# Source order for TensorE and the sync DMA queue in the last four stages, and for all engines in gate and up

## The chip, the core and the metric

The kernel runs on one core of a Trainium2 chip. The core has a matrix engine (TensorE, PE; its weight loads are shown as PEld), a vector engine (VectorE, DVE), a scalar engine (ScalarE, ACT), a general engine (GpSimd, POOL), and a sync engine (SP) that issues DMAs; 16 DMA engines move the data. ScalarE can issue DMAs too. Every engine has its own instruction queue, and instructions wait on semaphores. TensorE's clock is granted at one of two levels, 1.2 and 2.4 GHz; the profile gives it as 0.5 to 1.0. The metric is the device time of one execution in microseconds, the median of several runs.

## The reference

One inference step of a one-layer encoder for 1024 frames of a new stream and 32 frames of a running one. `layer` does, for all 1056 token rows together:

```python
u = rmsnorm(x, norm_mix_g) @ w_in                       # 1024 -> 4616 columns
cy = silu(layernorm(depthwise_causal(a * sigmoid(gl)))) @ w_conv_pw
ao = attend(q, k, v, logf).reshape(B, T, 512) @ w_attn_o
mixed = sigmoid(g_conv) * cy + sigmoid(g_attn) * ao
h = x + mixed @ w_out                                   # 1024 -> 1024
z = rmsnorm(h, norm_ffn_g)
h = h + (silu(z @ w_gate) * (z @ w_up)) @ w_down        # 1024 -> 2816 -> 1024
```

and at the end a last rmsnorm. All inputs are float32.

## The kernel before

**Arithmetic.** Each float32 operand is kept as a rounded half "hi" (cast by ScalarE) and a difference "lo" (subtracted by VectorE or GpSimd; the helper is `split`, lines 237 and 240). A product is three matmuls: hi by hi, hi by lo, lo by hi.

**Stages.** (1) input projection, convolution, attention and `mixers` (the convolution's projection and its gate; results go to the DRAM tile `md`). (2) `attn_out`: attention's projection, 8 blocks of 128 output columns, each for 4 chunks of 264 token columns: 12 matmuls per block and chunk, then a multiplication by the gate read from `gd` (L1455), an addition of `md` (L1457), and a split into `mh`, `ml`. (3) `out_proj`: the output projection in two pairs of chunks, 8 blocks each; after a pair's blocks, `pair_operand` (a generator, advanced step by step) sums the squares by a matmul with ones (L1528), computes the norm (L1529 to L1535), scales h (L1547, four operations for each quarter), forms sums of quarters (L1555), and splits them into the seven operands `zh`, `zl` of that pair. (4) `ffn_up`: 22 units of 128 hidden columns. Gate and up of one unit are a two by two block product that is done as seven products (a Strassen-like scheme in the orders `ORDER` and `EARLY`), 12 matmuls of 264 columns each (L1603), 84 matmuls for a unit and pair, 3696 in all. The seven weight operands of the next unit are prepared beside it (`unit_weights`: a sum `ws`, L1577, then a split into `whl`). Unit 0 is done for pair 0 first and for pair 1 last. (5) `ffn_down`: the down projection, 352 columns a matmul, reading the hidden values back from `hidd`; its last part also writes the output rows.

**Seven products.** `ORDER` is 1, 5, 2, 6, 7, 3, 4; products 1, 5 and 2 are copied out of their PSUM banks by ScalarE (L1606) and their banks are used again by products 7, 3 and 4, so that product 7 waits for the copy of product 1. GpSimd adds two of the copies (L1609, L1610), VectorE adds the rest (L1612 to L1618); a Silu on ScalarE and a multiplication on VectorE (L1661 to L1664) finish each half, and a DMA writes it (L1666).

**What sets the order.** The instructions are traced in source order; a planner then orders each engine's queue by priorities and by the times that it expects, and places tiles in memory. `high_priority` moves instructions forward. Inside `manual_schedule(engines=...)` the named engines keep the source order. Before the change that holds for TensorE from attention up to the end of `mixers` (the `region` that `mixers` closes); from `tokens_in_pairs` on the planner orders every queue, with one matmul pinned by `keep_in_program_order` (L1528). Memory of stages 2 to 4 lies over that of stage 1, and stage 5's over that of 2 to 4, so a first tile of a stage may wait until an old one is given up.

**Buffers that matter.** Seven PSUM banks for products and one for the ones matmul in stages 2 to 4; pool `first` (14 tiles of 4 by 264 columns), `second` (16), `passing` (8 smaller ones); 4 + 6 tiles for weight operands; two tiles for the sums `ws`; four raw weight tiles, two of which (`raw`) stay across stages.

Of the kernel before, what the change touches and what calls it, by code (L numbers as in the profile page):

```python
# [15 lines left out]
P = 128  # L16
NP = 1024
# [38 lines left out]
EARLY = (1, 5, 7, 4, 3, 2, 6)  # L56
BANK = {1: "a", 5: "b", 2: "c", 6: "d", 7: "a", 3: "b", 4: "c"}
# [79 lines left out]
class Builder:  # L137
# [223 lines left out]
    def jobs(self):  # L361
# [951 lines left out]
    def mixers(self, region):  # L1313
# [5 lines left out]
        def gated(j):  # L1319
# [25 lines left out]
    def tokens_in_pairs(self):  # L1345
# [11 lines left out]
        self.start_queue([cols(rows(I["w_attn_o"][0]), j) for j in range(8)] +  # L1357
                         [cols(rows(I["w_out"][0]), j) for _ in range(2) for j in range(8)], 4)
# [57 lines left out]
    def attn_out(self):  # L1416
# [3 lines left out]
        self.fetch(3)  # L1420
        w = self.block()

        def loads(j):
            out = [self.Q(self.pa, s="gate") for _ in range(2)]
            for x, src in zip(out, (self.gd[1, j], self.md[j])):
                nc.sync.dma_start(x.rearrange("p c n -> p (c n)"), src)
            return out

        oh = {}
        for c in range(4):  # L1430
            x = self.Q(self.pa, s="o")
            e = min(CW, NP - CW * c)
            with self.tc.high_priority(400):
                nc.sync.dma_start(x[:, :, 0:e], self.od[:, :, CW * c:CW * c + e].rearrange("a p n -> p a n"))
            if e < CW:
                nc.vector.tensor_copy(x[:, :, e:CW], self.os)
            oh[c] = self.Q(self.pa, FR, "oh"), self.Q(self.pa, FR, "ol")
            self.split(x, *oh[c], nc.vector)
        x = None
        mx = {}  # L1440
        nxt = loads(0)
        for j in range(8):
# [4 lines left out]
            if (1, j) in late:  # L1447
                nc.scalar.activation(g, g, AF.Sigmoid)
            for p in range(2):
                if j % 2 == 0:  # L1450
                    mx[p, j // 2] = self.Q(self.pb, FR, "mh"), self.Q(self.pb, FR, "ml")
                for c in (2 * p, 2 * p + 1):
                    ps = self.psd()
                    self.block_products(ps, wj, lambda k: (oh[c][0][:, k, :], oh[c][1][:, k, :]), CW)
# [9 lines left out]
    def out_proj(self, w):  # L1464
# [53 lines left out]
        for self.unit in self.ahead:  # L1518
            pass
# [450 lines left out]
```

## Time and profile before

| | us |
|---|---|
| median of 3 runs | 1581.76 (1579.77 to 1582.91) |
| profiled execution, its own time | 1584.55 |
| its span, first to last instruction | 1582.8 |
| TensorE busy in the span | 1513.3 (96%) |
| weight loads | 1474.0 (93%) |
| VectorE busy | 1013.0 (64%) |
| ScalarE busy | 594.7 (38%) |
| GpSimd busy | 509.7 (32%) |
| granted clock, mean | 0.986 |

The profile is of one execution. Busy times of the engines overlap. A matmul's end is modelled, and matmuls overlap in the records, so that an interval between starts says more than a duration. A wait is the idle time of an engine before an instruction, with what released it in brackets. The stages of the change lie between about 657 us and the end.

### The profile page before, as it was taken

What the parts mean: (1) busy time and instruction counts of PE and PEld (TensorE: products, weight loads), DVE (VectorE), ACT (ScalarE), POOL (GpSimd) and SP (SyncE); (2) the same over time, 40 slices, a digit from 0 to 9 for tenths busy, and PEclk for the clock granted to TensorE, in tenths of its full rate; (3) what the DMA queues carried; (4) which work ended last, traced back from release to release, by engine and by line L of the source; (5) the groups of instructions that cost most, each with busy time, mean ns of one, the idle gap of its engine ahead of it and who ended that gap; (6) DMA issues with size and microseconds to landing.
All of it is one profiled execution on the core that took longest, in us unless ns stands there. A gap on an engine that the chain in (4) does not pass through costs nothing.

```text
span 1582.8 us, 27182 instructions
## 1 busy us (share of the span) xinstructions
PE 1513.3 (96%) x10622; PEld 1474.0 (93%) x10622; DVE 1013.0 (64%) x1742; ACT 594.7 (38%) x1220; POOL 509.7 (32%) x473
## 2 busy tenths in 40 slices
PE   8999999989999999899997999999999989999997
PEld 7999998979999998789997999999999989999996
DVE  7799998668776565267499655555555545442226
ACT  4412212376655444243455333333333334121115
POOL 2200000433432221210004566676666661122221
PEclk9999999999999999989999999999999999999999
DMA  8312332434634377685641222222222228321113
GB/s 249 119 41 80 91 100 78 122 88 136 196 106 114 109 239 221 193 261 166 181 140 44 79 82 78 78 77 65 70 81 82 81 75 324 111 83 51 42 63 110
DMA packets 209711, 186.18 MB, mean 118 GB/s; under 512 B 12587, under 2 KB 186567, under 8 KB 209584
## 3 DMA queue, kind: packets, MB, share of 16 engines
q1 hardware_dynamic: 209567, 184.46, 37.6%
q8 instruction: 83, 1.36, 0.3%
q14 instruction: 45, 0.36, 0.1%
q10 hardware_dynamic: 16, 0.00, 0.0%
HBM read 131.41 MB, written 53.01 MB: 117 GB/s over the span
## 4 chain that ended last, share of the span: by engine, by line
PE 56%; DVE 10%; POOL 5%; ACT 4%; issue 3%; DMA 2%; SPq 0%; ACTq 0%; DVEq 0%; POOLq 0%
PE pd L1413 18%; PE pd L1603 17%; PE pd L418 11%; POOL whl L240 4%; DVE ws L1577 2%; PE po L1101 2%; PE ps L1062 2%; PE pt L1084 2%; PE pd L1751 1%; DVE h L1547 1%; POOL t L1609 1%; PE pt L243 1%; DVE zl L240 1%; ACT whl L237 1%; PE pd L1776 1%
## 5 line engine op out<-in xcount | busy, mean ns | idle before, releaser
L1603 PE MATMUL pd<-zh,whl 128*128 128x264 f32 x2464 | 457.4, 286 | 15.0 <-ACT t L1606 7.3
L1603 PEld LDWEIGHTS pd<-zh,whl 128*128 128x128 f32 x2464 | 384.8, 189 | 19.9 <-ACT t L1606 11.6
L1603 PE MATMUL pd<-zl,whl 128*128 128x264 f32 x1232 | 351.1, 285 | 0.6 <-DVE zl L240 0.6
L418 PE MATMUL pd<-xl,whi 128*128 128x352 f32 x832 | 270.6, 325 | 0.5 <-POOL xl L528 0.5
L418 PE MATMUL pd<-xh,whi 128*128 128x352 f32 x832 | 271.0, 326 | 0.0
L418 PE MATMUL pd<-xh,wlo 128*128 128x352 f32 x832 | 270.9, 326 | 0.0
L1603 PEld LDWEIGHTS pd<-zl,whl 128*128 128x128 f32 x1232 | 233.0, 189 | 0.9 <-DVE zl L240 0.9
L240 POOL TENSOR_TENSOR wlo<-raw,whi 128x640 fp32r<-128x640 f32 (+2 forms) x55 | 102.9, 1872 | 244.3 <-ACT whi L237 194.6
L240 POOL TENSOR_TENSOR whl<-ws,whl 128x512 fp32r<-128x512 f32 x105 | 143.5, 1382 | 114.0 <-ACT whl L237 114.0
L237 ACT CAST whi<-raw 128x1024 fp32r<-128x1024 f32 (+2 forms) x78 | 70.2, 900 | 235.6 <-PE pd L1413 111.2
L418 PEld LDWEIGHTS pd<-xl,whi 128*128 128x128 f32 x832 | 156.8, 188 | 1.9 <-POOL xl L528 0.8
L418 PEld LDWEIGHTS pd<-xh,whi 128*128 128x128 f32 x832 | 156.8, 189 | 1.4 <-issue 0.2
L418 PEld LDWEIGHTS pd<-xh,wlo 128*128 128x128 f32 x832 | 156.8, 188 | 0.7
L755 DVE SCALAR_TENSOR_TENSOR acc<-cu,wdw,acc 128x1024 f32<-128x1024 f32 x120 | 147.2, 1278 | 0.2
L1727 DVE TENSOR_TENSOR h<-pd,h 128x352 f32<-128x352 f32 x96 | 49.8, 522 | 134.7 <-PE pd L1413 134.3
L1413 PE MATMUL pd<-hl,whi 128*128 128x352 f32 x360 | 116.1, 323 | 0.0
L1413 PE MATMUL pd<-hh,whi 128*128 128x352 f32 x360 | 116.1, 322 | 0.0
L1413 PE MATMUL pd<-hh,wlo 128*128 128x352 f32 x360 | 116.1, 322 | 0.0
L237 ACT CAST whl<-ws 128x512 fp32r<-128x512 f32 x115 | 71.2, 620 | 96.0 <-DVE ws L1577 70.4
L1609 POOL TENSOR_TENSOR t<-t,t 128x264 f32<-128x264 f32 x44 | 43.6, 991 | 165.5 <-ACT t L1606 165.5
L1046 POOL TENSOR_SCALAR_AFFINE_SELECT cr<-cr 128x128 f32<-128x128 f32 x64 | 25.7, 401 | 160.7 <-DVE s L1069 83.2
L948 POOL TENSOR_TENSOR v<-vt,v 128x256 fp32r<-128x256 f32 x16 | 12.0, 772 | 201.3 <-DVE v L947 201.3
(341 smaller groups left out, 3133.4 us busy)
## 6 DMA issues: line engine op xcount, KB each, us to landing
raw<-in_w_in SPq DMA_DIRECT2D x35, 512.0 KB, 4.0
hidd<-y SPq DMA_DIRECT2D x44, 264.0 KB, 2.0
hid<-hidd SPq DMA_DIRECT2D x18, 528.0 KB, 4.3
gd<-gate SPq DMA_DIRECT2D x48, 176.0 KB, 1.8
q<-qd SPq DMA_DIRECT2D x32, 256.0 KB, 5.1
raw<-in_w_down SPq DMA_DIRECT2D x24, 320.0 KB, 3.3
raw<-in_w_gate SPq DMA_DIRECT2D x12, 512.0 KB
raw<-in_w_up SPq DMA_DIRECT2D x12, 512.0 KB
```

Of the source, the lines that this page charges most:

```text
L237: nc.scalar.copy(hi, src)
L240: (lo_engine or nc.gpsimd).tensor_tensor(lo, src, f32(hi), ALU.subtract)
L418: nc.tensor.matmul(ps[:, :n], lhs, b, start=(m == 0), stop=(m == total - 1))
L755: nc.vector.scalar_tensor_tensor(acc[:, 0:NP], cu[:, j:j + NP], w(j), acc[:, 0:NP], op0=ALU.mult, op1=ALU.add)
L1062: nc.tensor.matmul(s[:, 512 * j:512 * j + e - o], q[:, m, qs], k[:, o:e], start=(m == 0), stop=(m == 1))
L1084: nc.tensor.transpose(t[:, o:o + P], lt[n, b][:, P * kb:P * kb + P], self.ident)
L1101: nc.tensor.matmul(o[:, 0:256], self.v[p][hh][:, kb, :], pt[:, m, r:r + 256], start=(kb == 0 and m == 0), stop=(kb == 2 * g + 1 and m == 1))
L1413: self.nc.tensor.matmul(ps[:, :n], a[:, k, :], b, start=(m == 0), stop=(m == total - 1))
L1577: nc.vector.tensor_tensor(src, q(terms[0]), q(terms[1]), terms[2])
L1603: nc.tensor.matmul(banks[b], x[:, k, :], y[:, k, :], start=first and k == m == 0, stop=last and k == 3 and m == 2, skip_group_check=True)
L1609: nc.gpsimd.tensor_tensor(t2, t2, t5, ALU.add)
L1727: nc.vector.tensor_add(s, ps[:, :CH], s)
```

## The change

It has five parts. (a) From `tokens_in_pairs` to the end, TensorE and SP keep the source order; in `ffn_up` all five engines do. (b) `attn_out` issues the four loads of attention's output first, takes three weight blocks at once, and goes through the chunks in the outer loop for those three blocks; the other five blocks go as before. Its first two weight blocks are loaded at the end of `mixers`, as two further entries of the list `L`; `dense` looks one block ahead for splits and three for loads, so it also splits block 0 and loads block 2, which `attn_out` then does again. (c) The last `md` writes (block 7) and the last `hidd` write are issued by ScalarE. (d) The preparation of a unit's weights is cut into steps `s` (the sum) and `p` (the split), placed between the seven products by the tables `STEPS`, and stands ahead of the copies and additions of the product just issued; the operands of pair 1 are advanced one step later than before. (e) Silu and multiplication stand right behind the products that they need.

```diff
+STEPS = {0: "s0", 1: "p0", 2: "s3", 3: "p3", 4: "s4", 5: "p4", 8: "s1", 9: "p1 s2", 10: "p2", 11: "p5", 13: "p6"}
+STEPS_0 = {0: "s0", 1: "p0 s1", 2: "p1 s2", 3: "p2 s3", 4: "p3 s4", 5: "p4 p5", 6: "p6"}
+STEPS_1 = {7: "s0", 8: "p0 s3", 9: "p3 s4", 10: "p4 s1", 11: "p1 s2", 12: "p2 p5", 13: "p6"}
...
-        w = I["w_conv_pw"][0].rearrange("(k p) n -> p k n", p=P)
-        for j in range(8):
-            L.append((w[:, :, P * j:P * j + P], 4))
+        for w in (I["w_conv_pw"][0], I["w_attn_o"][0]):
+            w = w.rearrange("(k p) n -> p k n", p=P)
+            for j in range(8):
+                L.append((w[:, :, P * j:P * j + P], 4))
...
-                nc.sync.dma_start(self.md[j, :, CH * c:CH * c + CH], x[c])
+                (nc.sync if j < 7 else nc.scalar).dma_start(self.md[j, :, CH * c:CH * c + CH], x[c])
...
+        for i in range(2):
+            self.raws[i] = self.raw.pop(n - 8 + i)
+        self.begun = 2
...
+        o = []
+        for c in range(4):
+            o.append(self.Q(self.pa, s="o"))
+            e = min(CW, NP - CW * c)
+            nc.sync.dma_start(o[c][:, :, 0:e], self.od[:, :, CW * c:CW * c + e].rearrange("a p n -> p a n"))
+        self.fetch(4)
...
+        ws = [self.block() for _ in range(3)]
+        gm = []
         for c in range(4):
+            x = o.pop(0)
+            if c == 3:
+                nc.vector.tensor_copy(x[:, :, NP - CW * c:CW], self.os)
             oh[c] = self.Q(self.pa, FR, "oh"), self.Q(self.pa, FR, "ol")
             self.split(x, *oh[c], nc.vector)
+            x = None
+            if c == 0:
+                gm = [loads(j) for j in range(3)]
+            for j in range(3):
+                products(j, ws[j], gm[j][0], c)
+                if c % 2:
+                    sums(j, *gm[j], c // 2)
+            if c == 2:
+                w = self.block()
...
-            self.tc.keep_in_program_order(nc.tensor.matmul(t[:, :CW], self.ones, acc[:, c, :], start=True, stop=True))
+            nc.tensor.matmul(t[:, :CW], self.ones, acc[:, c, :], start=True, stop=True)
...
+        def prep(steps):
+            for step in steps.split():
+                at = int(step[1])
+                i = ORDER[at]
+                terms = A_SUMS[i]
+                a = [r[b][:, 4 * h:4 * h + 4, :] for b, h in terms[:2]]
+                if step[0] == "s":
+                    if len(terms) > 1:
+                        sums[i] = self.sums.tile([P, 4, P], F32, tag="s", name=self.name("ws"))
+                        nc.vector.tensor_tensor(sums[i], a[0], a[1], terms[2])
+                else:
+                    t = pools[at].tile([P, KD, P], FR, tag="w", name=self.name("whl"))
+                    out[i] = t[:, 0:4, :], t[:, 4:8, :]
+                    self.split(sums.pop(i, a[0]), *out[i], lo_engine)
...
+            between()
+            if i in copies:
                 nc.scalar.copy(copies[i], banks[b])
...
             if i == 3:
-                nc.vector.tensor_tensor(t1, banks["b"], t1, ALU.add)
+                nc.scalar.activation(y1, banks["b"], AF.Silu)
+                add(t1, banks["b"], t1)
+                nc.vector.tensor_mul(y1, t1, y1)
             if i == 4:
-                nc.vector.tensor_tensor(t2, banks["c"], t2, ALU.add)
-            between()
+                add(t2, banks["c"], t2)
+                nc.scalar.activation(y0, t2, AF.Silu)
+                nc.vector.tensor_mul(y0, banks["c"], y0)
...
+            steps = (STEPS_0, STEPS_1, STEPS)[min(n, 2)]
+            step = 0
             for p in (0, 1) if 0 < n < NFF else (n > 0,):
-                step = 0
 
                 def between():
                     nonlocal w, step
+                    if prep and step in steps:
+                        w = prep(steps[step])
                     step += 1
-                    w = next(ahead, w)
-                    if n < 2 and p == 0 and n + step > 1:
+                    if n < 2 and p == 0 and n + step > 2:
                         next(work, None)
...
+                queue = nc.scalar if n == NFF else nc.sync
+                queue.dma_start(self.hidd[f, :, o:o + 2 * CW], y.rearrange("p c n -> p (c n)"))
...
+        E = mybir.EngineType
+        region.enter_context(self.tc.manual_schedule(engines={E.PE, E.SP}))
         self.tokens_in_pairs()
         self.out_proj(self.attn_out())
+        region.close()
+        region.enter_context(self.tc.manual_schedule(engines={E.PE, E.SP, E.Activation, E.DVE, E.Pool}))
         self.ffn_up()
+        region.close()
+        region.enter_context(self.tc.manual_schedule(engines={E.PE, E.SP}))
         self.ffn_down()
+        region.close()
```

## Rows read from the trace of the kernel before

**Rows 1.** Source view: line, operation, count, ns min/median/max, first and last start.

```profile
L1413 PE MATMUL pd<-oh,whl x256: 278/283/586, 663.7 to 724.1; 128*128 128x264 f32 x128
...
L1603 PE MATMUL pd<-zh,whl x2464: 278/283/557, 824.7 to 1301.4; 128*128 128x264 f32 x190
```

**Rows 2.** Windows: stretch, length, busy (count) by engine, clock, DMA share, GB/s.

```profile
677.90:684.00 6.10, 5.99 (x28) 6.00 (x29) 2.56 (x6) 1.07 (x1) 0.00 (x0) 0.52 1.00 380
...
690.00:724.00 34.00, 34.00 (x283) 34.00 (x282) 27.32 (x44) 18.08 (x24) 6.42 (x4) 1.00 0.84 257
724.00:731.00 7.00, 3.71 (x28) 3.29 (x27) 6.90 (x13) 1.87 (x3) 0.00 (x0) 1.00 0.05 15
...
824.70:876.80 52.10, 41.41 (x306) 39.83 (x305) 48.31 (x68) 27.06 (x48) 20.24 (x15) 0.93 0.18 57
876.80:1276.50 399.70, 392.47 (x3195) 388.49 (x3193) 229.16 (x328) 141.21 (x323) 263.80 (x209) 1.00 0.24 75
1276.50:1301.50 25.00, 24.91 (x204) 24.89 (x204) 9.80 (x19) 10.19 (x24) 18.09 (x16) 1.00 0.22 73
1301.50:1306.80 5.30, 0.20 (x3) 0.01 (x1) 1.00 (x4) 0.96 (x3) 0.00 (x0) 0.83 0.69 211
1306.80:1311.60 4.80, 4.80 (x15) 4.53 (x16) 3.81 (x8) 3.62 (x8) 0.00 (x0) 0.50 0.97 314
```

**Rows 3.** Timeline of SP's queue at the start of `attn_out` (start, length, instruction).

```profile
657.30 0.43 SPq L1434 DMA_DIRECT2D o<-od  x1
663.55 0.32 SPq L1327 DMA_DIRECT2D md<-gate  x1
...
673.07 0.49 SPq L1434 DMA_DIRECT2D o<-od  x1
```

**Rows 4.** Timeline of ScalarE and GpSimd there, with the wait before.

```profile
662.21 1.07 ACT L237 CAST oh<-o 128x1056 fp32r<-128x1056 f32 x1 [5.46 <-DMA o<-od]
...
667.60 1.26 POOL L240 TENSOR_TENSOR whl<-rawx,whl 128x512 fp32r<-128x512 f32 x1 [12.14 <-ACT whl L237]
```

**Rows 5.** Timeline of VectorE at the change to `out_proj`.

```profile
724.10 0.69 DVE L1577 TENSOR_TENSOR ws<-raw,raw 128x512 f32<-128x512 f32 x1 [2.04 <-DMA raw<-in_w_up]
```

**Rows 6.** Timeline of TensorE: the ones matmuls of pair 0.

```profile
779.62 0.71 PE L1528 MATMUL pt<-sq,ones 128*128 128x264 f32 x2
782.86 0.68 PE L1528 MATMUL pt<-sq,ones 128*128 128x264 f32 x2
```

**Rows 7.** Timeline of one unit in gate and up: VectorE, ScalarE, VectorE, TensorE.

```profile
996.85 3.47 DVE L1577 TENSOR_TENSOR ws<-raw 128x512 f32<-128x512 f32 x2 [0.82 <-POOL whl L240]
...
1002.60 0.92 ACT L1606 COPY t<-pd 128x264 f32<-128x264 f32 x3
1002.72 0.43 DVE L1664 TENSOR_TENSOR y<-pd,y 128x264 f32<-128x264 f32 x1 [0.49 <-ACT y L1662]
1003.01 0.39 PE L1603 MATMUL pd<-zh,whl 128*128 128x264 f32 x1 [0.36 <-ACT t L1606]
```

**Rows 8.** Timeline of VectorE: the first operation of pair 1's norm.

```profile
835.92 0.73 DVE L1533 SCALAR_TENSOR_TENSOR na<-na,nr 128x528 f32<-128x528 f32 x1 [0.45 <-ACT nr L1532]
```

**Rows 9.** Timeline of VectorE in pair 0's operands.

```profile
790.12 2.11 DVE L1547 SCALAR_TENSOR_TENSOR h<-h,vec,nr 128x264 f32<-128x264 f32 x5
...
794.84 1.25 DVE L1555 TENSOR_TENSOR sum<-h,h 128x1056 f32<-128x1056 f32 x1
...
797.37 1.24 DVE L240 TENSOR_TENSOR zl<-sum,zh 128x1056 fp32r<-128x1056 f32 x1
```

**Rows 10.** Groups of GpSimd, 876.8 to 1276.5: busy us, mean ns, idle before.

```profile
L240 POOL TENSOR_TENSOR whl<-ws,whl 128x512 fp32r<-128x512 f32 x95 | 128.2, 1366 | 93.2 <-ACT whl L237 93.2
```

**Rows 11.** Timeline of SP's queue at the end of gate and up.

```profile
1303.11 0.34 SPq L1666 DMA_DIRECT2D hidd<-y  x1
1303.54 5.79 SPq L1699 DMA_DIRECT2D hid<-hidd  x12
```

**Rows 12.** Timeline of VectorE in the last part: an output row.

```profile
1551.27 1.41 DVE L1849 SCALAR_TENSOR_TENSOR y<-ps,s,gf 128x512 f32<-128x512 f32 x2
```

More of the change, by code (lines that the diff above doesn't have):

```diff
@@ L1419, in attn_out @@
         late = set(self.late)
-        self.fetch(3)
-        w = self.block()
+        o = []
[4 more added lines that the diff above has]
+        self.fetch(4)
         def loads(j):
-            out = [self.Q(self.pa, s="gate") for _ in range(2)]
+            out = [self.Q(pool, s="gate") for pool in (self.pa, self.pb if j < 3 else self.pa)]
@@ L1425, in loads, with products @@
             for x, src in zip(out, (self.gd[1, j], self.md[j])):
                 nc.sync.dma_start(x.rearrange("p c n -> p (c n)"), src)
+            if (1, j) in late:
+                nc.scalar.activation(out[0], out[0], AF.Sigmoid)
             return out
         oh = {}
-        for c in range(4):
[L1431 to L1436, printed above, removed]
+        def products(j, w, g, c):
+            ps = self.psd()
+            self.block_products(ps, w, lambda k: (oh[c][0][:, k, :], oh[c][1][:, k, :]), CW)
+            nc.vector.tensor_mul(g[:, c, :], ps[:, :CW], g[:, c, :])
@@ L1443, in attn_out @@
+        ws, gm = None, None
+        nxt = loads(3)
+        for j in range(3, 8):
             (g, m), wj = nxt, w
@@ L1446, in attn_out @@
             w = self.block()
[L1447 to L1454, printed above, removed]
-                    nc.vector.tensor_mul(g[:, c, :], ps[:, :CW], g[:, c, :])
-                cs = slice(2 * p, 2 * p + 2)
-                nc.vector.tensor_add(g[:, cs, :], g[:, cs, :], m[:, cs, :])
-                b = 2 * (j % 2)
-                hi, lo = (x[:, b:b + 2, :] for x in mx[p, j // 2])
-                self.split(g[:, cs, :], hi, lo, nc.vector)
+            for c in range(4):
+                products(j, wj, g, c)
+                if c % 2:
+                    sums(j, g, m, c // 2)
+            g = m = None
         self.mx = mx
@@ L1509, in out_proj @@
             if n in (1, 2, 3, 4, 5, 6):
-                self.unit = next(self.ahead)
+                prep(f"s{n - 1} p{n - 1}")
             if j == 7:
@@ L1516, in out_proj @@
                 work = self.pair_operand(p, h, acc, (EARLY, ORDER)[p])
-        first = None
-        for self.unit in self.ahead:
-            pass
-        self.work = work
+        self.unit, self.work = prep("p6"), work
     def pair_operand(self, p, h, acc, order):
@@ L1597, in seven_products @@
                 banks[b] = self.psd()[:, :CW]
-            last = i not in copies
             hi, lo = w[i]
-            zh, zl = z[i]
+            zh, zl = self.z[p][i]
             for k in range(4):
-                for m, (x, y) in enumerate(((hi, zh), (hi, zl), (lo, zh))):
-                    nc.tensor.matmul(banks[b], x[:, k, :], y[:, k, :], start=first and k == m == 0,
-                                     stop=last and k == 3 and m == 2, skip_group_check=True)
-            if not last:
+                for m, (x, z) in enumerate(((hi, zh), (hi, zl), (lo, zh))):
+                    nc.tensor.matmul(banks[b], x[:, k, :], z[:, k, :], start=first and k == m == 0,
+                                     stop=i not in copies and k == 3 and m == 2, skip_group_check=True)
+            between()
+            if i in copies:
                 nc.scalar.copy(copies[i], banks[b])
```

73 lines of the change are left out of this document (32 added, 41 removed).

## The prediction, made before the result was known

> **What bounds the kernel now.** I read the busy shares first: TensorE is busy for 96% of the span, so only its waits and its time at the lower clock can be won. Second comes the source view of two matmul lines, which gives the stages: attention's projection runs from 663.7 to 724.1, gate and up from 824.7 to 1301.4 [rows 1]. Third come windows cut at TensorE's gaps [rows 2]. In each the reader compares the length with the number of matmuls times an undisturbed interval. That interval is 34.00/283 = 0.120 us in the projection and 25.00/204 = 0.1225 us in gate and up. What is lost:
> - Projection: 8 blocks x 4 chunks x 12 = 384 matmuls are worth 46.1 us of 60.4, so 14.3 are lost, part of them at half clock (0.52, the 1.2 GHz level, from 677.9 to 684.0).
> - Change to `out_proj`, 724 to 731: 28 matmuls are worth 3.4 us of 7.0, so 3.6.
> - Start of gate and up: the two later windows hold 19 units of 168 and 204 matmuls, so 3696 - 3396 = 300 fall in the first 52.1 us. They are worth 36.8; 15.3 are lost (the ones matmuls included).
> - The 19 units: 399.7 - 3192 x 0.1225 = 8.7 lost, 0.46 a unit.
> - Before `ffn_down`: 5.3 of no work, and 4.8 at clock 0.50, half of which is lost: 7.7.
>
> Together 49.6 us, and no edit here can give more. Fourth, timelines show what stands in which queue; these are taken part by part.
>
> **A. Projection, chunk by chunk.** Now SP issues the first load of attention's output at 657.30, then stands until it can issue the last `md` write at 663.55, and the fourth load goes at 673.07 [rows 3]. After, the four loads stand in a row and those writes are ScalarE's. I let the first go when it goes now: its cast starts at 662.21 [rows 4], its lo half is done some 2.5 us later, and TensorE goes on 1.0 later than its first product now. The four loads are 2.1 MB, 8.2 us at 257 GB/s [rows 2], so chunk 1 is there by the time it is wanted. The third weight block comes behind them: at about 667 instead of in time for the split at 667.60 [rows 4], split by 670; two blocks of chunk 0 last 2.9 us, so TensorE waits 2.4. The six gate loads (3.2 MB, 8.5 to 12.6 us at 380 or 257 GB/s [rows 2]) follow; seven PSUM banks hold 10 us of products until the first multiplication needs one, and I take 1.0 of waiting. Loss 4.4 in place of 14.3: **+9.9**. Upper bound 13.3 (only the first 1.0). Lower bound 2: if the memory is not free before the queue's next step now, 663.55, all loads go 6.3 later, and the third block and the gates each hold TensorE up. The unused split (about 0.6 ScalarE, 1.26 GpSimd) falls in GpSimd's idle 12.14 before 667.60; the unused load is 0.26 MB, 1 us of a queue. ScalarE's writes wait for VectorE's products, behind which only chunk casts stand, and ScalarE has 5.46 of idle there [rows 4].
>
> **B. Change to `out_proj`.** VectorE stands 2.04 us for `w_up` with the sums of unit 0 while the projection's last gates queue behind it [rows 5]. In source order the two loads go right behind the last gates, ahead of further weights, and TensorE takes the last two chunks between pair 0's sums and their use. VectorE is still ordered by the planner. **+2.5** of 3.6; bounds 3.6 and -2.0 (one such wait more).
>
> **C. Ones matmuls of pair 0.** Now 3.24 us lie between the two, filled with products [rows 6]; in source order nothing stands between, and one bank serves both. **-2.5** (3.24 less the 0.71 of work); bounds 0 and -3.2. Behind the waiting matmul stands the rest of `out_proj`.
>
> **D. Gate and up.** The 0.46 a unit: two `ws` on VectorE take 3.47 and wait for GpSimd to give back a sums tile; the previous half's additions stand behind them, its Silu behind those, the three copies behind the Silu, and product 7 waits 0.36 for a copy [rows 7]. With the steps placed by source, copies stand behind one short cast, and I find no wait in the steady units: GpSimd has 7 x 1.37 [rows 10] and four additions of about 1, some 14 of 20.6 us. So 8.7 is won there.
>
> The start pays for it. Let T0 be the first product, a product 1.47 us. The ones matmuls stand after the third product and hold TensorE for 2.5 + 1.3. VectorE's norm starts 11.2 after the first product now (835.92 [rows 8]); the same table loads and reads stand before it, so T0+11.2. Then its source order has, ahead of unit 0's last addition: 3 norm steps of 0.73, 7 weight operations of 0.69 [rows 5], 8 scalings of 0.42, a sum 1.25, the cast it waits for 1.07 [rows 4], two splits of 1.24 [rows 9], 4 product operations of 0.43 [rows 7]: 16.9, T0+28.1. Addition, Silu and copy take 1.2, and only at T0+29.3 may product 7 of unit 1 start; TensorE got there at 11 x 1.47 + 3.8 = 20.0 and waits 9.3. The second list, up to the copy in unit 1's second half, is Silu and multiplication 0.85, cast and split 2.3, 8 scalings 3.4, three times sum, cast and split 10.7, five product operations 2.2, Silu and multiplication 0.85, sum, cast and copy 2.6: 22.9 from T0+28.5, so T0+51.4, while TensorE arrives at 29.3 + 7 x 1.47 = 39.6: 11.8. Then 2.4 at half clock, as after the gap of 5.3 now [rows 2], and about 2 for unit 2's second weight block, whose preparation begins late. Sum 29.3 against 15.3 + 8.7 = 24.0 now: **-5.3**. Bounds: +8.7 if the start loses only what it does now; -15 if VectorE's lists run a third longer, as beside a busy GpSimd, where a `ws` of 0.69 [rows 5] takes 1.73 [rows 7].
>
> **E. Change to `ffn_down`.** SP holds the twelve loads of hidden values behind the last `hidd` write (1303.11, the loads from 1303.54 [rows 11]), though they read units 1 to 4. After, that write is ScalarE's. When the tiles come free is not shown: between 0 (loads no earlier) and 7.7 (TensorE goes straight on). The write waits for the last half, 9 to 10 us behind the one before, so I take more than half: **+4.5**.
>
> **F. Last part.** TensorE now takes row transposes when they are ready. In source order they stand in the queue, and each output row holds its PSUM pair until two operations of 1.41 in total have read it [rows 12]. **-1.0**; bounds 0 and -4.2 (three rows, one such read each).
>
> Sum: 9.9 + 2.5 - 2.5 - 5.3 + 4.5 - 1.0 = +8.1. The profiled execution took 1584.55 (1.75 outside its span), so 1576.4 in its terms; it is 2.8 above the median of runs, and 1581.76 - 8.1 = **1573.7**.
>
> **A rule weighed.** The `md` write holds SP from 657.73 to 663.55 [rows 3], so what ScalarE's queue saves there is the stand. The Trainium skill (DMA: Bandwidth & Descriptors, "Issuing engines are not separate DMA queues") says that DMAs issued from several engines run on the same 16 DMA engines, and that a second issuing engine saves only the issuing time. By that rule the writes on ScalarE give four issues of 0.32 to 0.34, 1.3 us, in place of A and E, and the sum would be about -5; the trace bears out the bandwidth half (380 GB/s at a DMA share of 1.00 [rows 2]) but not that issue time is all.
>
> **Rivals.**
> 1. Slower: steady units bound by GpSimd and VectorE. Source order fixes sum, cast and difference of the second and third block late in a unit. For it: two `ws` take 3.47 beside GpSimd [rows 7]. Against: at the means of [rows 10] the blocks are done with some 4 us to spare. It decides when seven differences and five sums, all at such lengths (7 x 1.9 + 5 x 1.73 = 22), exceed the 20.6 of a unit: then 1.4 to 1.6 a unit, 19 units, 28 us: 1602.
> 2. The loads go no earlier, because tiles, not queues, hold them: A at 2, E at 0.3: 8.1 - 7.9 - 4.2 = -4: 1586. For it: the loads of [rows 3] are spread over 16 us; against: the stand before 663.55 is the queue's own.
> 3. The start loses no more than now, since unit 2's weights are no longer prepared in it: 14 more, 1559.7. Against: the lists above.
> 4. The start's lists run as beside a busy GpSimd, D at -13: 1581.4.
> The change not doing what it says is rival 2.
>
> **How the numbers follow.** Forecast 0.53, rivals 1 to 4: 0.07, 0.12, 0.14, 0.14. The forecast's own range, from C, E and half of A's and D's bounds, is 1567 to 1580. A measurement tells 0.2%, 3.2 us, from no change: bounds 1578.6 and 1584.9. Faster: 0.47 + 0.14 + 0.04 (rival 4) + 0.02 (rival 2) = 0.67; same 0.06 + 0.07 + 0.04 = 0.17; slower 0.16. The range 1560 to 1587 leaves out rival 1, half of 3 and a third of 2, 0.18.
>
> **What would show it.** A: four loads in a row on SP near 657, `attn_out` 50 to 51 us long, no half clock. B: less than 2 us idle before the first out product. C: 2 to 3 us before the second ones matmul. D: no wait on L1606 from unit 3 on, 20.6 a unit, and two waits of about 9 and 12 us before product 7 in unit 1. E: hidden loads before the last product of gate and up has ended. Wrong would be: loads of attention's output still after 663, waits every 20.6 us, or a start of gate and up with no long wait.

## The result, and the profile after

The changed kernel took 1590.59 us (median of 4 runs, 1589.57 to 1593.29) against 1582.34 for the kernel before (4 runs beside it, 1579.77 to 1584.52): ratio 1.0055, 95% interval 1.0035 to 1.0075. It is 8.3 us slower where 8.1 faster was forecast, and lies above the range. The two profiled executions differ by 6.5 us (spans of 1582.75 and 1589.26); that is what the stages account for.

| stretch, us (from the first starts of its matmuls) | before | after | forecast gain | measured gain |
|---|---|---|---|---|
| first product of attention's projection, at | 663.66 | 664.91 | in A | -1.25 |
| projection | 60.58 | 55.68 | A with its start +9.9 | +4.90, A +3.65 |
| output projection, to the first ones matmul | 55.38 | 53.01 | B +2.5 | +2.37 |
| from there to gate and up | 45.07 | 50.34 | C -2.5 | -5.27 |
| gate and up | 476.72 | 479.38 | D -5.3 | -2.66 |
| gap, and down projection to its last part | 227.82 | 228.22 | E +4.5 | -0.40 |
| last part | 43.81 | 48.06 | F -1.0 | -4.25 |
| rest | 9.70 | 9.66 | | +0.04 |
| sum | | | +8.1 | -6.5 |

In these two executions B came out as forecast and D 2.6 better; A, E, C and F are worse by 6.3, 4.9, 2.8 and 3.3.

Each column is one execution, and the first three stages differ from one execution to the next. Nine kernels below (banks, behind, normlate, planner2, lastp, hidpool, hidsp, hidmem, hidmemp) have the source of the projection as it is in after. In them the projection took 55.5 to 58.2 us and the output projection up to the first ones matmul 53.4 to 56.5; from there to gate and up it took 47.6 to 49.2 in the eight of them without the edit of banks. Against the one profile of the kernel before, B is then -1.1 to +2.0, C is -2.5 to -4.1, and the projection gains 2.4 to 5.1. So the table shows the best end of B, nearly that of the projection, and the worst of C. The other stages repeat better: where their code is as in after, gate and up took 479.3 to 479.4, the gap with the down projection 227.6 to 228.8, and the last part 48.1, or 49.6 with a stretch at half clock.

Windows of the changed kernel by stage (stretch, length, busy time and count of PE, PEld, DVE, ACT, POOL, granted clock, DMA share, GB/s):

```profile
664.90:720.60 55.70, 50.55 (x385) 50.03 (x386) 37.34 (x59) 24.07 (x31) 11.15 (x7) 0.94 0.78 251
720.60:773.60 53.00, 50.49 (x411) 49.86 (x409) 33.25 (x53) 19.60 (x33) 0.00 (x0) 1.00 0.51 154
773.60:823.90 50.30, 47.82 (x364) 47.20 (x365) 40.02 (x60) 24.59 (x36) 0.00 (x0) 0.93 0.56 169
823.90:892.90 69.00, 45.11 (x320) 43.63 (x319) 48.30 (x69) 28.38 (x50) 15.88 (x14) 0.83 0.10 30
892.90:1303.40 410.50, 410.50 (x3384) 410.49 (x3383) 185.38 (x342) 155.06 (x342) 245.09 (x224) 1.00 0.27 78
...
776.00:782.90 6.90, 6.12 (x26) 5.91 (x27) 1.92 (x3) 3.50 (x6) 0.00 (x0) 0.51 0.01 3
853.40:858.00 4.60, 4.60 (x21) 4.60 (x22) 3.80 (x6) 1.45 (x3) 2.07 (x2) 0.50 0.79 225
876.10:881.90 5.80, 5.80 (x26) 5.80 (x27) 4.36 (x5) 2.11 (x5) 3.51 (x3) 0.50 0.01 3
1310.70:1315.30 4.60, 4.60 (x14) 3.94 (x15) 3.25 (x7) 2.75 (x7) 0.00 (x0) 0.50 0.91 298
```

Against [rows 2]: the later units (fifth line) run without a gap, 410.5/3384 = 0.1213 us a matmul, and all of gate and up's loss sits in the fourth line. The last four lines are stretches at half clock, each behind a wait; two more of 3.4 us lie in the projection (666.8 and 677.1, clock 0.50). Together 28.7 us, of which half, 14, is lost. TensorE's waits in the changed kernel (who waited for whom: total us, times, longest):

```profile
PE pd L1637 <- ACT t L1641: 19.9, 2, 10.2
...
PE pd L1421 <- DVE ol L244: 5.1, 2, 4.2
PE pt L1553 <- ACT nr L1555: 4.9, 2, 2.5
PE pd L1421 <- ACT hh L241: 4.7, 3, 2.4
...
PE ps L247 <- DVE y L1883: 2.7, 1, 2.7
PE pd L1421 <- ACT oh L241: 2.1, 1, 2.1
PE pd L1421 <- ACT mh L241: 2.0, 1, 2.0
```

The two largest are product 7 of unit 1, both pairs. The others have their causes in the next rows. **Projection**, timelines of SP, ScalarE and VectorE:

```profile
656.59 2.55 SPq L1432 DMA_DIRECT2D o<-od  x4
659.24 0.69 SPq L1387 DMA_DIRECT2D rawx<-in_w_attn_o  x1
666.94 0.37 SPq L1387 DMA_DIRECT2D rawx<-in_w_attn_o  x1
667.36 1.81 SPq L1438 DMA_DIRECT2D gate<-gd  x1
...
656.80 6.94 ACTq L1332 DMA_DIRECT2D md<-gate  x2
663.78 1.07 ACT L241 CAST oh<-o 128x1056 fp32r<-128x1056 f32 x1 [7.17 <-DVE o L1465]
...
672.39 0.43 DVE L1448 TENSOR_TENSOR gate<-pd,gate 128x264 f32<-128x264 f32 x1 [6.25 <-DMA gate<-gd]
675.12 0.43 DVE L1448 TENSOR_TENSOR gate<-pd,gate 128x264 f32<-128x264 f32 x1 [2.29 <-DMA gate<-gd]
675.47 3.59 DVE L244 TENSOR_TENSOR ol<-o,oh 128x1056 fp32r<-128x1056 f32 x3
```

The four loads do stand in a row. But ScalarE now stands at the `md` write, and its first cast, at 662.21 before [rows 4], is queued behind it. SP stands from 659.93 to 666.94 before the load of the fourth weight block, and the gates wait behind that; VectorE's multiplications wait for the gates, and the lo half of chunk 1 is queued behind them: TensorE's 4.2.

**Change to `out_proj`, ones matmuls, change to `ffn_down`, last part**: VectorE; TensorE; SP and ScalarE; TensorE.

```profile
720.16 0.69 DVE L1606 TENSOR_TENSOR ws<-raw,raw 128x512 f32<-128x512 f32 x1 [2.49 <-DMA raw<-in_w_up]
...
773.60 0.71 PE L1553 MATMUL pt<-sq,ones 128*128 128x264 f32 x2
776.78 1.25 PE L1553 MATMUL pt<-sq,ones 128*128 128x264 f32 x2 [2.48 <-ACT nr L1555]
...
1304.59 7.88 SPq L1733 DMA_DIRECT2D hid<-hidd  x11
1305.03 0.33 ACTq L1701 DMA_DIRECT2D hidd<-y  x1
1305.47 0.48 ACT L241 CAST hh<-hid 128x352 fp32r<-128x352 f32 x1 [0.94 <-DVE y L1657]
...
1549.86 0.65 PE L247 MATMUL ps<-ident,h 128*128 128x128 f32 x4 [1.46 <-ACT y L1846]
1555.49 0.61 PE L247 MATMUL ps<-ident,h 128*96 128x128 f32 x4 [2.66 <-DVE y L1883]
```

VectorE still stands for `w_up` [rows 5], 2.49 us; the second ones matmul waits 2.48; of the twelve loads of hidden values one goes at 1295.73, the other eleven from 1304.59 on, no earlier than before [rows 11]; and TensorE stands before two row transposes.

### The profile page after: what moved, and what is told of

The parts are those of the page before. It is cut to its first block, busy times and chain, and to the rows that moved or that the text cites. A ratio compares the mean times of both kernels' runs of the same rounds, so it can differ in the third digit from the quotient of the medians.

```text
span 1589.3 us, 27289 instructions
## 1 busy us (share of the span) xinstructions
PE 1511.0 (95%) x10622; PEld 1474.7 (93%) x10622; DVE 957.5 (60%) x1742; ACT 601.3 (38%) x1221; POOL 473.8 (30%) x474
## 3 DMA queue, kind: packets, MB, share of 16 engines
HBM read 131.67 MB, written 53.01 MB: 116 GB/s over the span
## 4 chain that ended last, share of the span: by engine, by line
PE 68%; DVE 6%; ACT 3%; DMA 2%; issue 2%; POOL 0%; SPq 0%; DVEq 0%; ACTq 0%; POOLq 0%
PE pd L1637 26%; PE pd L1421 21%; PE pd L423 11%; PE po L1106 2%; PE pt L1089 2%; PE ps L1067 2%; PE pd L1785 1%; DMA gate<-gd 1%; PE pt L247 1%; PE pd L1810 1%; DVE h L1572 0%; PE pt L1268 0%; DVE ml L244 0%; ACT zh L241 0%; DVE zl L244 0%
## 5 line engine op out<-in xcount | busy, mean ns | idle before, releaser
L1637 PE MATMUL pd<-zh,whl 128*128 128x264 f32 x2464 | 454.5, 286 | 21.5 <-ACT t L1641 19.9
L1627 DVE TENSOR_TENSOR t<-pd,t 128x264 f32<-128x264 f32 x176 | 75.4, 429 | 207.0 <-POOL t L1645 158.1
L244 POOL TENSOR_TENSOR whl<-ws,whl 128x512 fp32r<-128x512 f32 x105 | 135.3, 1289 | 156.7 <-ACT whl L241 156.7
L1761 DVE TENSOR_TENSOR h<-pd,h 128x352 f32<-128x352 f32 x96 | 49.2, 522 | 133.7 <-PE pd L1421 131.9
L1644 POOL TENSOR_TENSOR t<-t,t 128x264 f32<-128x264 f32 x44 | 34.4, 782 | 156.5 <-ACT t L1641 156.5
L1641 ACT COPY t<-pd 128x264 f32<-128x264 f32 x132 | 49.7, 379 | 74.2 <-PE pd L1637 74.0
```

Source lines behind the costliest of these rows:

```text
L244: (lo_engine or nc.gpsimd).tensor_tensor(lo, src, f32(hi), ALU.subtract)
L1627: add = lambda out, a, b, op=ALU.add: nc.vector.tensor_tensor(out, a, b, op)
L1637: nc.tensor.matmul(banks[b], x[:, k, :], z[:, k, :], start=first and k == m == 0, stop=i not in copies and k == 3 and m == 2, skip_group_c ...
L1641: nc.scalar.copy(copies[i], banks[b])
L1644: nc.gpsimd.tensor_tensor(t2, t2, t5, ALU.add)
L1761: nc.vector.tensor_add(s, ps[:, :CH], s)
```

## Experiments

Each is an edit of the changed kernel ("after"). Where no interval is given, the kernel ran once.

### Projection and output projection: gates, banks

```diff
-        self.fetch(4)
+        self.fetch(3)
```

> The changed kernel with the fourth weight block of attention's projection loaded behind the first six gate loads instead of ahead of them. Theory (one waiting load holds the queue): in the changed kernel SP stood from 659.9 to 666.9 before that load, whose memory VectorE had not given back; the gates, behind it in the queue, came at 667.4 to 671, VectorE's first two multiplications waited 6.25 and 2.29 us for them, and the lo half of chunk 1 stood behind these, for which TensorE waited 4.23 us and then ran 3.4 us at half clock. Then the gates go near 660, the 4.23 and its half clock go, and the projection takes about 49.8 us instead of 55.7. Rival (the transfers themselves are too slow, since four loads of attention's output and six gates are 5.3 MB): the wait stays above 2 us and the projection stays above 53.

The projection took 50.69 us, well below the 55.5 to 58.2 of the kernels without this edit: the 4.2 is gone, the theory holds. But the output projection took 107.41 instead of 103.35, and gate and up began at 823.17, only 0.8 earlier; the time was 1592.28. TensorE's row at the change, and VectorE's ahead of it:

```profile
723.20 0.59 PE L1421 MATMUL pd<-mh,whi 128*128 128x264 f32 x1 [4.70 <-ACT mh L241]
...
718.00 0.69 DVE L1606 TENSOR_TENSOR ws<-raw,raw 128x512 f32<-128x512 f32 x1 [3.15 <-DMA raw<-in_w_up]
```

The planner put the sum for unit 0 ahead of the projection's last sums on VectorE, and it waits for `w_up`. What one stage wins, the next one waits for, until that sum is moved (the kernel combined, below).

```diff
-            t = self.pst()
+            t = self.psd() if c else self.pst()
```

> The changed kernel with a second PSUM bank for the second ones matmul of each pair. Theory (the single bank makes the wait, and the wait lowers the clock): the waits of 2.48 us in the output projection and 2.42 us in gate and up go, and with the first of them the stretch at half clock from 776.0 to 782.9, in which some 6 us of products took twice as long; the output projection falls from 103.4 to about 98 us, gate and up by 2.4 more at most. Rival (the second matmul waits for the sums of squares or for ScalarE's Ln anyway): both waits stay above 1 us and nothing moves.

From the first ones matmul to gate and up 44.82 us instead of 50.34, at clock 1.00: the wait and its half clock were all of C. The stage took 101.28, not 98, since it had a wait of 3.1 and a half-clock stretch ahead of the ones matmuls. The stage alone would not show the edit (hidmem, without it, took 100.99); the part behind the ones matmuls does, since no kernel with after's code there was under 47.5. In gate and up the second wait went too (478.08). Time 1589.00.

What the wait costs differs by the clock behind it. Windows of 6.9 us from the second ones matmul of pair 0 in lastp, hidsp and after, each behind the same wait of 2.48 us:

```profile
778.40:785.30 6.90, 6.83 (x54) 6.77 (x55) 3.17 (x5) 4.26 (x7) 0.00 (x0) 1.00 0.00 0
```
```profile
781.00:787.90 6.90, 6.89 (x42) 6.77 (x43) 3.13 (x5) 4.26 (x6) 0.00 (x0) 0.75 0.00 0
```
```profile
776.70:783.60 6.90, 6.82 (x31) 6.61 (x32) 2.52 (x4) 3.33 (x6) 0.00 (x0) 0.55 0.00 0
```

TensorE does 54, 42 or 31 matmuls in the same time. The stretch from the first ones matmul took 47.57, 49.10 and 50.34: the wait cost 2.8, 4.3 or 5.5 us against banks. Which of the three comes is not explained.

### Start of gate and up: behind, normlate, planner2

behind: `between()` moved from ahead of the copies to the end of the loop's body, in units 0 and 1.

> The changed kernel with the preparation steps and pair 1's operands of units 0 and 1 placed behind the copies and additions of the product instead of ahead of them. Theory A (the prediction's: a copy that stands behind the lists holds product 7): both waits of 9.7 and 10.2 us before product 7 go, and gate and up fall from 479.4 to about 460. Theory B (VectorE is the bound of the start: it is idle for only about 13 of 53 us there, and all operands of pair 1 are its work): the waits move to the products of unit 1's pair 1, which wait for their operands, and gate and up fall by no more than 5 us.

Gate and up took 479.85 and the two waits 17.1 (6.47 and 10.66): theory A's 460 falls, and B's bound holds. But the waits did not move to pair 1's products, as B says; both still stand before product 7, for a copy. The edit puts each step behind the copies of its own product; those of unit 1 still stand behind all steps of unit 0. A queue in which they stand ahead of these was not run.

```diff
         nc.scalar.activation(r, r, AF.Exp, scale=-0.5)
+        for _ in range(2 * p):
+            yield
```

> The changed kernel with pair 1's norm on VectorE two products later in the source order of unit 0, so that two weight steps of unit 1 come ahead of it. Theory (VectorE bounds the start, and the 5.12 us for which it stands before the norm are lost for good): the stand goes below 2 us, pair 1's last operand is ready some 4 us sooner, and gate and up take about 475 instead of 479.4. Rival (the order of the copies, not VectorE's work, makes the waits): the two waits before product 7 keep their sum of 19.9 within 1 us.

479.15: nothing won, the theory falls. VectorE no longer stands before the norm, but 5.91 us at 839.25 for a weight cast, which is queued behind the norm's six operations on ScalarE (832.55 to 838.44, two table loads of 1.28 among them). The rival's sum did not hold as stated (5.38 + 11.86 = 17.2 instead of 19.9); with two new waits of 0.9 at pair 1's first product it is 19.1.

planner2: `region.enter_context(manual_schedule(...all engines))` at `n == 2` instead of ahead of `ffn_up`.

> The changed kernel with units 0 and 1 of gate and up ordered by the planner again, on all engines; source order begins with unit 2. Theory (the fixed lists of the start are what gate and up lose, the fixed steps of later units are what it wins): no wait in the later units, the start loses about 15 to 17 us as in the kernel before instead of 26.6, and gate and up take about 468 to 470 us instead of 479.4. Rival (VectorE's work alone bounds the start, whoever orders it, because the sums of unit 2 now fall into it): gate and up stay above 476.

464.12, 15.3 less than after and 12.6 less than before; time 1579.43. Its start loses 464.1 - 3696 x 0.1213 = 15.8, as the kernel before's (52.1 - 300 x 0.1213 = 15.7 [rows 2]), and its later units nothing: theory right, by more than it said. Windows of 53 us from the first product, in after, behind, normlate, planner2 and before:

```profile
823.90:876.90 53.00, 30.71 (x225) 29.81 (x224) 37.51 (x56) 21.62 (x34) 4.19 (x4) 0.82 0.11 33
```
```profile
825.50:878.50 53.00, 32.62 (x229) 31.66 (x228) 37.85 (x58) 21.92 (x35) 4.57 (x4) 0.81 0.11 33
```
```profile
827.50:880.50 53.00, 31.47 (x227) 30.08 (x226) 37.07 (x57) 21.64 (x34) 5.03 (x4) 0.81 0.11 33
```
```profile
827.10:880.10 53.00, 43.66 (x314) 41.55 (x313) 48.14 (x67) 28.23 (x49) 21.11 (x17) 0.94 0.17 53
```
```profile
824.70:877.70 53.00, 42.31 (x313) 40.73 (x312) 49.21 (x69) 27.06 (x48) 21.08 (x15) 0.94 0.18 56
```

In all three fixed orders VectorE (busy time: third number) stands for 15 to 16 of 53 us, in the planner's orders for 4 to 5, and TensorE gets 84 to 89 matmuls more done. Of the 15.5 us in after, 5.1 are before pair 1's norm, 2.5 for the last product of the output projection, and 6.6 are six stands of 0.8 to 1.2 before a difference, for its cast on ScalarE: sum, cast and difference follow each other with nothing between. In planner2 VectorE has no stand of 0.7 us or more before a difference of pair 1's operands, it has other work there. So it is not the amount of VectorE's work (48.1 us of it are done in planner2's window, 37.5 in after's) but the fixed order. planner2 frees all five queues of the two units at once; which of them it takes is not shown.

### Last part: lastp

Source order closed ahead of `last_part`.

> The changed kernel with source order on TensorE and SP ended ahead of the last part of the down projection. Theory (TensorE stands before row transposes, because an output row holds its PSUM pair until two operations of VectorE have read it): the waits of 1.46 and 2.66 us go, the last part takes 43.8 us as in the kernel before instead of 48.1, and the whole is 4.2 us shorter. Rival (the rows are late because the stage before ended otherwise, not because of the order): the last part stays above 46.

43.87 us, without the two waits; time 1585.25. F was this order alone.

### Change to `ffn_down`: hidpool, hidsp, hidmem, hidmemp

```diff
-                queue = nc.scalar if n == NFF else nc.sync
+                queue = nc.gpsimd if n == NFF else nc.sync
```

> The changed kernel with the last write of hidden values issued by GpSimd, which has nothing else to do then, instead of ScalarE. Theory (ScalarE's first cast of hidden values stands behind that write, which waits for VectorE's last multiplication): the first cast, at 1305.47, comes 1 to 5 us earlier, and the 2.7 us before the down projection become less than 1.5. Rival (memory: the second and third load of hidden values wait until ScalarE, VectorE and the write have given back their tiles, 1304.6 and 1307.9): the loads are issued when they were, TensorE waits again between 1308 and 1311, and the first stretch of the down projection ends as late as before.

> The changed kernel with the last write of hidden values back on SP, ahead of the twelve loads, as in the kernel before. Theory (memory holds the loads, and the queue that holds the write does not matter): from the last product of gate and up to the last part of the down projection it takes 228.2 us in the changed kernel (2.7 and 225.5) and stays within 1.5 of that. Rival (the prediction's term E: the write's stand on SP is what the move wins): 230.5 or more.

The gap and the down projection together took 228.0 and 227.7 (after 228.2, before 227.8). In hidpool the gap fell from 2.7 to 1.8, but the loads went no earlier and TensorE waited behind it instead, as the rival says: who issues the write changes nothing by itself. Times 1592.90 and 1593.45.

```diff
-        t, s, y = self.D("t"), self.D("t"), self.D("y")
+        D = (lambda s: self.Q(self.pa, s=s)[:, 0:2, :]) if last else self.D
+        t, s, y = D("t"), D("t"), D("y")
```

> The changed kernel with the sums and the result of the last half of gate and up in tiles of another pool, so that the first loads of hidden values no longer lie over them. Theory (memory): the loads are issued in a row behind 1296, eight or more of the twelve before the last product ends, TensorE has no further wait between its first matmul of the down projection and the end of the stretch, and the gap and the down projection together take 222 to 224 us instead of 228.2. Rival (ScalarE's casts behind the last Silu): the loads go early, but the casts still begin 2.1 us behind the last product and follow each other with VectorE's differences; the sum falls by less than 2 us.

> As hidmem, with the last write on GpSimd. Theory (memory alone): within 0.7 us of hidmem. Rival (ScalarE's queue matters once the memory is free): the gap before the down projection falls from 2.7 to below 2, and the sum by 1 us more than in hidmem.

224.5, just above what was expected, and 221.2; times 1584.75 and 1585.44 (each ran once, and hidmemp lost its 3.2 in earlier stages and in the last part). SP's loads in hidmem (from 1300 on; seven had gone by 1296.5) and in hidmemp:

```profile
1304.54 2.22 SPq L1734 DMA_DIRECT2D hid<-hidd  x5
```
```profile
1295.53 5.62 SPq L1734 DMA_DIRECT2D hid<-hidd  x12
```

Memory was the first cause: the early loads lay over the last half's sums and result. Once it is free, the write's queue counts as well, as the rival of hidmemp says. ScalarE's first cast of hidden values in hidmem, where its write goes at 1302.49, and in hidmemp:

```profile
1302.94 2.81 ACT L241 CAST hh<-hid 128x352 fp32r<-128x352 f32 x7 [0.94 <-DVE y L1658]
```
```profile
1304.21 4.73 ACT L241 CAST hh<-hid 128x352 fp32r<-128x352 f32 x12
```

Behind the start of the last product (1300.79 and 1303.09) that is 2.15 and 1.12 us. The gap was 2.7 in hidmem and 1.8 in hidmemp, and only hidmem had half clock behind it (0.50 from 1305.1 to 1308.5, so 1.7 lost): 2.6 of the 3.2.

SP's eighth load was held too, as its waits in hidmem show (who waited for whom: total us, times, longest):

```profile
SPq L1734 <- DMA hidd<-y: 8.1, 1, 8.1
```

It went 2.05 us behind the issue of ScalarE's write. It does not read that write: in hidmemp the same load goes at 1298.82, ahead of the write at 1305.07. In hidmem's trace the write and the eighth load tell of their landing by the same semaphore (106), and the load waits for that semaphore before it goes; in hidmemp the eighth load's is another one (105), which is free by then. The views do not print semaphores; the traces hold them. TensorE has no further wait over 0.3 us in hidmem, so that this cost it little.

### The pieces together

combined has gates, banks and lastp, and

```diff
-                (nc.sync if j < 7 else nc.scalar).dma_start(self.md[...], x[c])
+                (nc.sync if j < 7 else nc.gpsimd).dma_start(self.md[...], x[c])
...
-        for r, src in zip(first, self.units[0]):    # ahead of the loop
+            if n == 0:                               # in it, behind block 0
+                for r, src in zip(first, self.units[0]):
...
-            if n in (1, 2, 3, 4, 5, 6):
-                prep(f"s{n - 1} p{n - 1}")
+            if 1 < n < 8:
+                prep(f"s{n - 2} p{n - 2}")
```

> The changed kernel with the edits of gates, banks and lastp together, and two more: the last three writes of the mixers issued by GpSimd instead of ScalarE, and the two weight loads of unit 0 one block later in the output projection, its steps one block later too. Theory: the first cast no longer stands behind a write and comes near 662, so that the projection starts 1 to 1.5 us earlier; it takes about 50 us; VectorE's first sum for unit 0 no longer stands in front of attention's last sums, and the 4.70 us that the kernel gates waited before the output projection become less than 1.5, so that the output projection takes about 97 us; the last part takes 43.9. Gate and up then begin near 811 instead of 823.9, and the whole is some 16 us shorter than the changed kernel. Rival (what one stage wins, the next one waits for, because VectorE or the transfers are the bound from the projection on): gate and up begin after 818.

Time 1576.87. The first cast is at 660.46, the first product at 662.71; projection 55.75, output projection 95.52, gate and up from 813.98, last part 43.91. Only the projection missed, and with it the start of gate and up by 3 us: the loads of gates now began at 659.3, but VectorE's first two multiplications still waited 4.49 and 3.00 us for them, and chunk 1's cast (667.24) stood behind the third weight block's.

> The edits of the kernel combined, and units 0 and 1 of gate and up ordered by the planner as in planner2. If the stages add up: the combined kernel's span of 1574.9 less the 14.3 us that gate and up lose in planner2 against it (478.4 to 464.1), so 1560.6 and a time near 1562.4, 20 us below the kernel before. Rival (pair 1's operands meet a busier VectorE, because the output projection now ends earlier): gate and up stay above 470 and the time above 1568.

best_b:

```diff
             nc.sync.dma_start(o[c][...], self.od[...])
+            if c == 1:
+                self.fetch(3)
-        self.fetch(3)
...
-                gm = [loads(j) for j in range(3)]
+                for i, d in enumerate((self.gd[1], self.md)):
+                    for j in range(3):
+                        nc.sync.dma_start(gm[j][i], d[j])
```

> As best_a, with two loads moved in attention's projection: the third weight block behind the second load of attention's output instead of the fourth, and the three gates of the first blocks ahead of the three md values. Theory (in the kernel combined, chunk 1's cast stood behind that weight block's, which landed at 666.7, and its lo half behind two multiplications that waited 4.49 and 3.00 us for gates): the wait of 3.10 us at 673.4 and the half clock behind it go, the projection takes 51 to 52 us instead of 55.8, and the time is 3 to 4 us below best_a. Rival (the transfers are the bound there, whatever their order): less than 1 us below best_a.

best_a: 1562.46, ratio 0.9870 (0.9852 to 0.9888); gate and up 465.33, the stages add up. best_b: 1555.96, ratio 0.9837 (0.9818 to 0.9856); projection 49.43 and 6.5 us below best_a, more than expected: so the order of the loads, not their amount, was the bound. Which of the two moves did it is not separated.

> As best_b, with the whole down projection ordered by the planner instead of its last part alone. Theory (memory bounds the start of the down projection and TensorE's order inside it does not matter): within 1.5 us of best_b. Rival (the planner's queue, which puts weight loads ahead of the loads of hidden values, starts them better): 2 us or more below best_b.

> As best_b, with the tiles of hidmem. Theory (memory): 3 to 6 us below best_b, whose time was 1555.96, so 1550 to 1553. Rival: within 1.5 us of best_b.

> As best_d, with the last write on GpSimd. Theory (memory alone): within 1 us of best_d. Rival (ScalarE's queue): 1 to 2 us below it.

best_c: 1556.84, 0.9845 (0.9827 to 0.9863), no difference to best_b. best_d: 1554.64, 0.9826 (0.9811 to 0.9840), 1.3 below best_b and so what its rival said, although the gap and down projection took 224.7 instead of 228.5, as its theory said. In its profiled run attention's projection began 2.1 later (in the four kernels with best_b's projection it begins between 662.4 and 664.5) and the output projection took 1.8 more, which is not explained. best_e: **1549.35, ratio 0.9796 (0.9781 to 0.9810)**, 32 us below before and 41 below after. That is 5.3 below best_d, more than either side expected. The two profiled runs differ by 7.6: 1.1 in the gap, 2.6 in the down projection, where best_d ran at half clock from 1278.0 to 1284.8 (0.50) and best_e did not, 0.9 in gate and up, and 3.1 by an earlier start of it, which is not the edit's. Windows of best_e: start of gate and up, later units, down projection:

```profile
807.60:870.00 62.40, 52.94 (x390) 50.92 (x389) 56.17 (x78) 31.98 (x58) 25.47 (x20) 0.95 0.18 56
870.00:1272.10 402.10, 402.10 (x3315) 401.90 (x3313) 179.41 (x333) 151.57 (x333) 239.34 (x218) 1.00 0.27 81
...
1272.10:1492.80 220.70, 219.22 (x1369) 218.96 (x1369) 81.55 (x163) 50.89 (x100) 56.52 (x34) 1.00 0.35 119
```

What is left is the start of gate and up: 464.2 - 3696 x 0.1213 = 15.9.

## Why the prediction was wrong, step by step

Of the forecast's signs, A's row of four loads, C's wait and all of D's were there; A's length and clock and E's early loads were not. The largest misses are A (6.3) and E (4.9).

**A, first step.** "I let the first go when it goes now: its cast starts at 662.21" failed: the load went 0.7 earlier, the cast 1.6 later. The argument that ScalarE has 5.46 of idle there overlooked that the idle time was the cast's own wait: a stand moved from SP's queue to ScalarE's stands ahead of the next thing on the path. combined shows it: with the write on GpSimd the cast is at 660.46, 3.3 earlier, of which the load's own issue (655.78) makes 0.8. From that issue to the cast it is 7.2 us in after and 4.7 in combined.

**A, gates.** "I take 1.0 of waiting" failed, and it is A's largest miss: 4.2. I counted the third weight block's load ahead of the gates, not the fourth's, which waits 7 us for memory; gates shows it. The prediction's "no half clock" also failed, twice 3.4 us, of which half is lost. The 2.4 taken for the third block did not come: TensorE has no such wait.

**B.** The size is luck, the mechanism wrong: the loads didn't go early enough and VectorE stood 2.49 for `w_up` instead of 2.04. What went is the half-clock stretch behind the wait (clock 1.00 to 773.6), and it went in this execution and in hidmem's; in eight other kernels with the same source here it came back (0.50 for 3.4 or 6.8 us), and the stretch took 54.6 to 56.5 against 55.38 before. gates and combined point to VectorE's place for the sum as the cause of the wait.

**C.** The wait is as forecast (2.48). The step that failed is the bound of 3.2, which left out the clock behind the wait: in after TensorE ran at half clock to 782.9, and C cost 5.27; banks gives it all back. In lastp, hidpool and hidmem, at full clock behind the same wait, the stretch took 47.6, which is the forecast 2.5 more than before.

**D.** Right in mechanism: product 7 of unit 1 starts at T0+29.4 and T0+52.2 for T0+29.3 and T0+51.4, behind waits of 9.67 and 10.20 for 9.3 and 11.8, with no wait in later units. The start lost 69.0 - 312 x 0.1213 = 31.2 (forecast 29.3), half clock behind both long waits instead of one; the later units won 12.8 instead of 8.7, since the undisturbed interval is 0.1213. The lists count VectorE's stands for ScalarE's casts as given; planner2 shows that another order fills them, and loses 15.8. The 1.73 behind D's lower bound is half of a merged row [rows 7]: the two `ws` of before took 1.29 and 1.78, with 0.4 between.

**E.** The step that failed is "though they read units 1 to 4": the loads wait for memory, not for data, and the last half of gate and up held that memory (hidsp, hidpool, hidmem). The bound of 0 was nearly the measured value (-0.40); "more than half" had no row behind it.

**F.** The step that failed is the choice of 1.0. The price was in the text as the bound: "three rows, one such read each", 4.2. There were two waits, 4.1 together, and lastp takes it back.

**The whole.** Rival 2 (tiles hold the loads, A at 2, E at 0.3, 1586) was nearest; with C and F at what they cost it gives 1592. But its condition held for E alone: A's four loads did go early, so that its A is near by luck. The terms were bounded one by one and added as if they missed independently; A's two steps and F, and the waits of B and C, have one cause in common: a queue kept in order, in which something that waits stands ahead of what the path needs. The rule of the Trainium skill (DMA: Bandwidth & Descriptors, "Issuing engines are not separate DMA queues") made the sum about -5 and so came nearer than the forecast. hidsp and hidpool agree with it, 228.0 and 227.7 against 228.2; combined (the cast 3.3 earlier) and hidmemp against hidmem (3.2 in the stretch) do not: there the place of the write in a queue counts, not its issue time. The row that the prediction reads for the bandwidth half (380 GB/s) does not bear on it, since SP issued those transfers alone. hidmemp against hidpool does: GpSimd's last write landed in 6.1 us among SP's loads (DMA share 0.92 from 1305 to 1312), in 2.5 beside few (0.36).

## What to carry to other kernels

Moving a DMA that waits to another engine's queue moves the stand: look at what is next in that queue, and whether it is on the path. A wait of TensorE of some 2 us can cost more than itself, since the clock may halve behind it; count both, as a range. A stage that differs by 2 to 5 us between executions of the same code can't be judged by one pair of profiles. Fix the order where engines have slack (the later units, 12.6 us won) and leave it free where, as in the start of gate and up, two engines hand the same operands back and forth; and before a load is counted early, ask which tile it lies over.

## What the runs showed of the hardware

Short waits were enough for half clock, but not always. In after, waits of 2.08 and 0.91 us at 664.9 and 666.2 were followed by 3.4 us at 0.50, while the 2.05 us at 725.4, in the output projection, were not (clock 1.00); behind 2.31 us at 728.7 in hidpool it was 0.50 from 729.2 to 732.6. Behind one and the same wait of 2.48 us there were 0, 3.4 or 6.8 us at half clock (lastp, hidsp, after: the windows at banks).

Writes issued by GpSimd landed late where other transfers ran: 5.6 us (median of 3, `md`) and 6.9 (`hidd`) in best_e, where SP's took 3.1 and 2.1. It need not be the engine: in hidpool, with few transfers beside it, GpSimd's write of `hidd` landed in 2.5. DMA issues of best_e, then of hidpool (count, KB each, median us from issue to landing):

```profile
hidd<-y SPq DMA_DIRECT2D x43, 264.0 KB, 2.1
...
md<-gate SPq DMA_DIRECT2D x15, 176.0 KB, 3.1
...
md<-gate POOLq DMA_DIRECT2D x3, 176.0 KB, 5.6
hidd<-y POOLq DMA_DIRECT2D x1, 264.0 KB, 6.9
```
```profile
hidd<-y POOLq DMA_DIRECT2D x1, 264.0 KB, 2.5
```
